# Two-layer hybrid backbone on one core: when weights are split, and when the mixer's residual is prepared

## The chip, the cores and the metric

One core of one Trainium2 chip runs the whole network in one launch. The metric is the device time of that launch in microseconds. Five engines work from queues of their own, each strictly in order: TensorE (PE; its weight loads are listed as PEld), VectorE (DVE), ScalarE (ACT), GpSimd (POOL) and SyncE (SP), whose queue issues all the DMA loads and stores of this kernel.

## The reference

A two-layer network over 512 latent tokens and 256 context tokens of width 1024, in float32. Layer 0 mixes with gated linear attention beside differential attention, layer 1 with a bidirectional state-space (SSD) mixer; each layer then has a SwiGLU feed-forward network (FFN) with 2816 hidden units. What matters here is the frame around the mixers:

```python
x = layer_norm(ALPHA * x + gm_x * mix_x, ln_g[layer, 0], ln_b[layer, 0])
x = layer_norm(ALPHA * x + gf_x * swiglu(x * (1.0 + scf_x) + shf_x, ffn_w_in[layer], ffn_w_out[layer]),
               ln_g[layer, 1], ln_b[layer, 1])
...
# end of the SSD mixer (layer 1; only latent tokens are needed there)
y = y.reshape(b, s, SSD_D_INNER) * jax.nn.silu(z.astype(F32))
return group_rms_norm(y, norm_w).astype(z.dtype) @ w_out
```

## The kernel before

**Products in three.** Each float32 matrix is kept as a high half (rounded to float32r, a form that TensorE multiplies faster) and a low half (the rest). A product is `mm3`: high by high, high by low, low by high. Activations are held in `R0` as such a pair, weights in `RW`. The weights are read from memory in 222 items of up to 128x1024, in the fixed order of the list `plan`. An item passes three stations:

- its load, a DMA of 512 KB, into one of three buffers of `RAW`;
- its *split*: ScalarE copies it into the high half (`RW<-RAW`, 128x1024), then VectorE or GpSimd subtracts that from the item to get the low half (`RW<-RAW,RW`);
- its use on TensorE, out of one of four buffers of `RW` (a pair of halves each).

`issue_loads` drives this. `wq` counts the items loaded, split (`issued`), `taken` by a step of the kernel and `freed` after their last product. An item may be loaded up to three ahead of the splits and split up to four ahead of what has been freed. In the kernel before, `issue_loads` runs at `free` alone, and it books every split that a free buffer allows at once. A step takes one item (a convolution's 128 columns, `cv`), two (a gate and up pair of the FFN, or the halves of `z`) or three or four (rows of an output matrix: `fo`, `ow`, `sw`).

**A planner orders the queues.** The kernel is not issued in program order. `Timing` keeps a clock for TensorE and, for VectorE (V), ScalarE (S), GpSimd (G), the DMA issues (Q) and the transfers (D), lists of booked stretches, with estimated costs. An operation is booked at the first room on its engine from the moment that its operands are ready, which may be up to 10 us before TensorE's clock; an L list keeps GpSimd apart from those VectorE operations that read two operands from SBUF. `either` books an elementwise operation on VectorE or GpSimd, wherever it ends sooner by the estimate. At `flush` all that was booked is issued in order of the planned time. So what is booked first gets the room, and what comes later in the program is placed around it. Every instruction is then listed under one line of the profile (L105), and tiles have to be told apart by names: `HB` is the big work buffer, `HX` and `l` (slots of the layer) hold smaller ones, `f` those of the FFN, `R` is the activations' pair, `PS` PSUM, `xres` the residual stream in memory, `acs_rows` the decay rows that layer 1 loads for every tile.

Dependent work beside the products runs as generators (`spawn`); `pump`, called after every `mm3`, advances those whose operands the planner holds ready, `need` those that must be done.

**Layer 1.** Its steps are written out by hand:

```python
ORDER1 = "b0 x0 z0 x1 z1 x2 b1 z2 x3 x4 o0 x5 z3 b2 z4 o1 z5 x6 b3 x7 z6 o2 p z7 o3"
```

`b` and `x` are projections with a convolution (B and C, or 256 channels of x), `z` the gate's projection of 256 columns, whose tanh and silu product (`SZ`) are booked at its end; `o` is a quarter of the output product over four tiles of 128 tokens, summed in `acc`. For each `x` a chain `y_tile` per tile builds the SSD output, gates it with `SZ`, and transposes it for `o`. `o3` does not sum but goes on, tile by tile, into the layer norm: `out_tile` calls `ln.last` (gate, add the prepared residual, statistics), then `ln.chain` normalizes, transposes and writes the tile into `R0` for FFN 1. What `ln.last` adds to is prepared by `ln.prep(t)`: load `x` of the tile from `xres` into a buffer (there is one for all four tiles), scale it by `ALPHA` on ScalarE, multiply `acc` by the gate, add the two. Those are two operations of 128x1024 in HB, both booked by `either`. In the kernel before, step `p` does this for all four tiles, ahead of `z7` and `o3`.

Of the kernel before, what the change touches and what calls it, by code (L numbers as in the profile page):

```python
# [15 lines left out]
ALU = mybir.AluOpType  # L16
# [8 lines left out]
NT = NTOK // P  # L25
# [193 lines left out]
def backbone(ctx: ExitStack, tc: tile.TileContext, ins: dict, out: bass.AP):  # L219
    nc = tc.nc  # L220
    tm = Timing(nc)
    V, S, G = tm.V, tm.S, tm.G
    dma = tm.dma
# [93 lines left out]
        return c  # L317

    def pump():
        going = True  # L320
        while going:
            going = False
            for c in list(chains):
                if c.ready <= tm.clock and c.can():
                    c.step()
                    going = True
                    break
# [35 lines left out]

    plan = []
    wgate = {}
    wq = {"loaded": 0, "issued": 0, "taken": 0, "freed": 0}
    wviews = {}

    def plan_cols(key, w, c0, n=P):
# [6 lines left out]
        for i in range(2):  # L376
            plan.append(((key, n, i), [(None, w[i * 512:(i + 1) * 512, c0:c0 + 256].rearrange("(k p) c -> p k c", p=P))], (4, 256)))

    def issue_loads(limit=None):
        limit = limit or len(plan)  # L380
        while wq["loaded"] < min(limit, wq["issued"] + 3):
            j = wq["loaded"]
            _, pieces, (a, b) = plan[j]
            rv = RAW[:, j % 3, 0:a * b].rearrange("p (a b) -> p a b", b=b)
            for sl, ap in pieces:
                dma(rv[:, :, sl] if sl is not None else rv, ap)
            wq["loaded"] += 1
        if wq["issued"] < min(limit, wq["freed"] + 4):
            j = wq["issued"]
            _, _, (a, b) = plan[j]  # L390
            r = RAW[:, j % 3, 0:a * b]
            i = j % 4
            hi, lo, hf = RW[:, i, 0:a * b], RW[:, 4 + i, 0:a * b], RWf[:, i, 0:a * b]
            if plan[j][0] in wgate:
                tm.either(r, r, wgate[plan[j][0]], ALU.mult)
            S.activation(hi, r, AF.Copy)
            tm.either(lo, r, hf, ALU.subtract)
            wviews[j] = hi.rearrange("p (a b) -> p a b", b=b), lo.rearrange("p (a b) -> p a b", b=b)
            wq["issued"] += 1
            issue_loads(limit)  # L400

    def take(key):
        j = wq["taken"]
        assert plan[j][0] == key, (plan[j][0], key)
        wq["taken"] += 1
        return wviews[j]

# [313 lines left out]
    def start(mslots):  # L721
# [19 lines left out]
        for q in range(2):  # L741
            load_x(q)
            for i in range(4 * q, 4 * q + 4):
                load_mod(i)
            if q == 0:
                for j in range(4):
                    src = mod_b[0, j % 2 * 1024:j % 2 * 1024 + 1024].rearrange("(h q c) -> q h c", h=2, q=2)[j // 2]
                    dma(MB[32 * j:32 * j + 2, :].rearrange("p (h c) -> p h c", h=2), src.partition_broadcast(2))
                for d in range(2):
                    dma(prm_r[106:110, d * 64:(d + 1) * 64], ins["gla_b_gate"][0, d].rearrange("(h c) -> h c", c=64))  # L750
                issue_loads(3)
        load_x(2)
        load_x(3)
        for i in range(8, len(slots)):
# [55 lines left out]
        for q in range(3):  # L810
            while quarter[0] <= q:
                need_one()
            if q == 2:
                tm.floor["Q"] = tm.busy["Q"][-1][1]
                issue_loads()
                gate_params()
                load_params()
# [549 lines left out]
    def layer1(lnin, lnc):  # L1367
# [385 lines left out]
        for op in ORDER1.split():  # L1753
# [8 lines left out]
            elif op == "p":  # L1762
                need(*xsc[7])
                scale_shift(1, 1, 2)
                ln.load_gates()
                for t in range(2, NT):
                    ln.prep(t)
            else:
                ws = [take(("sw", 4 * i + k)) for k in range(4)]
                for t in range(2, NT):  # L1770
                    need(mxs[2 * i + 1])
                    need(yc[2 * i, t], yc[2 * i + 1, t])
                    out_tile(i, ws, t, t == NT - 1)
                    if i == 3:
                        outs[t] = spawn(ln.chain(t))
                        outs[t].step()
# [56 lines left out]
```

## Time and profile before

| | us |
|---|---|
| median of 3 runs (lowest, highest) | 2034.73 (2030.9, 2034.9) |
| the profiled execution | 2033.6 |
| its span, first to last instruction | 2031.7 |
| PE busy | 1921.0 |
| DVE busy | 1352.5 |
| ACT busy | 783.8 |
| POOL busy | 224.5 |

The times of the profile are those of the profiled execution, counted from its first instruction. Its stages are: layer 0 to about 510 (its start to 85), FFN 0 to about 1078, layer 1 to about 1650, FFN 1 to the end. An engine that is not the last to be waited for may idle at no cost; PE's idle time is what a gain has to come from.

### The profile page before, as it was taken

Reading aid. Unit: us, or ns where it says so; the run is one execution under the profiler, and the core shown is the slowest. Engines: PE = TensorE matmul, PEld = TensorE weight load, DVE = VectorE, ACT = ScalarE, POOL = GpSimd, SP = SyncE. Lnnn points to the kernel's source line nnn. Section 1 sums busy time; section 2 is a strip of 40 time slices with the busy share of each in tenths; the row PEclk is TensorE's granted clock in tenths of the full one; section 3 lists DMA queues with packets and bytes.
Section 4 is the critical chain, followed back from the end, with each engine's and each line's share of the span. In section 5 each row is a group of like instructions: output and inputs, shape, how many; then the busy total and the mean of one; then the engine's idle time right before and its main releaser. Section 6 shows DMA issues by size and latency. Waiting matters only on the chain.

```text
span 2031.7 us, 27248 instructions
## 1 busy us (share of the span) xinstructions
PE 1921.0 (95%) x10660; PEld 1650.1 (81%) x10660; DVE 1352.5 (67%) x2065; ACT 783.8 (39%) x1494; POOL 224.5 (11%) x281
## 2 busy tenths in 40 slices
PE   7999999997899999999998999999899789999997
PEld 4878787966899989899886888788788678888886
DVE  4765645588815656666478988977978884444456
ACT  3523135445423122212135465655546443222232
POOL 0100000021300000000113321401102230000010
PEclk9999999999999999999998999999999799999999
DMA  8433411122424434434323432233333325333331
GB/s 284 126 126 115 138 42 32 53 63 73 147 72 145 137 113 147 134 114 154 105 78 101 105 91 87 73 89 89 102 96 94 116 82 173 97 103 94 94 119 58
DMA packets 233071, 216.37 MB, mean 107 GB/s; under 512 B 18869, under 2 KB 202807, under 8 KB 232943
## 3 DMA queue, kind: packets, MB, share of 16 engines
q1 hardware_dynamic: 232943, 214.64, 34.4%
q8 instruction: 83, 1.36, 0.3%
q14 instruction: 45, 0.37, 0.1%
HBM read 204.94 MB, written 9.67 MB: 106 GB/s over the span
## 4 chain that ended last, share of the span: by engine, by line
PE 75%; DVE 14%; issue 3%; DMA 3%; ACT 3%; POOL 1%; SPq 0%; POOLq 0%; DVEq 0%; ACTq 0%
PE PS L105 75%; DVE HB L105 8%; DVE RW L105 2%; ACT HB L105 2%; DVE l L105 1%; DMA HB<-acs_rows 1%; DVE LNS L105 1%; ACT RW L105 1%; DMA HB<-in_x_dram 1%; DVE HX L105 1%; DVE sml L105 0%; SPq L105 0%; POOL HB L105 0%; DVE R L105 0%; POOL LNS L105 0%
## 5 line engine op out<-in xcount | busy, mean ns | idle before, releaser
L105 PE MATMUL PS<-R,RW 128*128 128x384 f32 (+3 forms) x5184 | 987.3, 349 | 19.9 <-DVE HB L105 5.8
L105 PEld LDWEIGHTS PS<-R,RW 128*128 128x128 f32 (+1 forms) x5184 | 887.3, 189 | 106.0 <-issue 20.6
L105 DVE TENSOR_TENSOR RW<-RAW,RW 128x1024 fp32r<-128x1024 f32 (+1 forms) x204 | 255.8, 1270 | 217.4 <-ACT RW L105 216.7
L105 ACT ACTIVATE RW<-RAW 128x1024 fp32r<-128x1024 f32 (+1 forms) x222 | 228.8, 1046 | 237.5 <-issue 174.5
L105 PE MATMUL PS<-RW,f 128*128 128x512 f32 x1320 | 304.7, 390 | 1.9 <-DVE RW L105 1.5
L105 ACT ACTIVATE HB<-PS 128x512 f32<-128x512 f32 (+4 forms) x247 | 129.8, 533 | 428.0 <-PE PS L105 409.7
L105 PEld LDWEIGHTS PS<-RW,f 128*128 128x128 f32 x1320 | 247.0, 188 | 55.0 <-DVE RW L105 2.1
L105 DVE TENSOR_TENSOR HB<-PS,HB 128x512 f32<-128x512 f32 (+2 forms) x276 | 160.2, 587 | 92.3 <-PE PS L105 88.7
L105 PE MATMUL PS<-RW,R 128*128 128x256 f32 (+1 forms) x1440 | 200.7, 298 | 5.4 <-DVE HB L105 4.1
L105 ACT ACTIVATE HB<-HB 128x128 f32<-128x128 f32 (+4 forms) x372 | 159.9, 488 | 102.6 <-DVE HB L105 67.5
L105 PEld LDWEIGHTS PS<-RW,R 128*128 128x128 f32 x1440 | 186.8, 196 | 14.1 <-DVE HB L105 4.9
L105 PE MATMUL PS<-RW,l 128*128 128x512 f32 x576 | 157.5, 415 | 15.5 <-DVE HX L105 6.8
L105 DVE TENSOR_TENSOR HB<-HB 128x256 f32<-128x256 f32 (+3 forms) x191 | 151.2, 802 | 21.8 <-ACT HB L105 16.3
L105 PE MATMUL PS<-HB 128*128 128x128 f32 (+6 forms) x896 | 147.2, 353 | 10.2 <-DVE HB L105 7.6
L105 PEld LDWEIGHTS PS<-RW,l 128*128 128x128 f32 x576 | 105.1, 192 | 45.5 <-DVE HX L105 8.2
L105 PEld LDWEIGHTS PS<-HB 128*128 128x128 f32 (+3 forms) x896 | 100.9, 188 | 42.5 <-DVE HB L105 12.7
L105 ACT ACTIVATE f<-HB 128x384 fp32r<-128x384 f32 (+2 forms) x68 | 37.4, 550 | 236.5 <-DVE HB L105 236.4
L105 POOL TENSOR_TENSOR HB<-HB 128x256 f32<-128x256 f32 (+1 forms) x55 | 72.8, 1334 | 504.8 <-DVE HB L105 336.1
L105 DVE TENSOR_TENSOR HB<-HB,PS 128x384 f32<-128x384 f32 (+2 forms) x68 | 39.7, 584 | 106.2 <-PE PS L105 106.2
L105 DVE SCALAR_TENSOR_TENSOR HB<-HB,CST 128x1024 f32<-128x1024 f32 x84 | 105.0, 1277 | 0.0
L105 DVE SCALAR_TENSOR_TENSOR HB<-HB,CW 128x770 f32<-128x770 f32 (+1 forms) x96 | 102.0, 1066 | 3.0
L105 PE MATMUL PS<-ident,HB 128*128 128x128 f32 x480 | 76.8, 288 | 22.5 <-DVE HX L105 11.5
(145 smaller groups left out, 1297.8 us busy)
## 6 DMA issues: line engine op xcount, KB each, us to landing
RAW<-in_ffn_w_in_dram SPq DMA_DIRECT2D x88, 512.0 KB
HB<-in_mod_w_dram SPq DMA_DIRECT2D x48, 512.0 KB
RAW<-in_ffn_w_out_dram SPq DMA_DIRECT2D x44, 512.0 KB
RAW<-in_ssd_w_in_dram SPq DMA_DIRECT2D x40, 512.0 KB
mod<-in_mod_w_dram SPq DMA_DIRECT2D x72, 256.0 KB
HB<-acs_rows SPq DMA_DIRECT2D x64, 256.0 KB
RAW<-in_ev_w_in_dram SPq DMA_DIRECT2D x20, 512.0 KB
RAW<-in_ssd_w_out_dram SPq DMA_DIRECT2D x16, 512.0 KB
```

The source lines that it names most:

```text
L105: f(*a, **k)
```

## The change

Two things change. First, `issue_loads` is also called by every `pump` and by `take`, and a split is booked only if `idle` finds, on the planner's lists, that VectorE has room for the low half by the time that the high half is done, or by now. Whatever `idle` says, an item is booked if it is one of the next two to be taken, and `take` books its own item. The limit of items (three during the start) becomes a field of `wq`. The loads are issued in the same function, so they follow the splits. Second, `ln.prep(t)` of layer 1's mixer moves from step `p`, where it stood for all four tiles, into `o3`, ahead of each tile's `out_tile`.

```diff
     def pump():
+        issue_loads()
         going = True
...
-    def issue_loads(limit=None):
-        limit = limit or len(plan)
-        while wq["loaded"] < min(limit, wq["issued"] + 3):
...
-        if wq["issued"] < min(limit, wq["freed"] + 4):
+    def idle(r, hi, lo):
+        n = math.prod(r.shape[1:])
+        c = [tm.COST[e][0] + tm.COST[e][1] * n for e in "SV"]
+        t = tm.room("S", max(tm.ready(r, 1), tm.free(hi, 1), tm.clock - 10.0), c[0]) + c[0]
+        t = max(t, tm.free(lo, 1))
+        return tm.room("V", t, c[1], True) <= max(t, tm.clock) + 0.1
+
+    def issue_loads(upto=0):
+        limit = wq["limit"]
+        while True:
+            while wq["loaded"] < min(limit, wq["issued"] + 3):
...
             j = wq["issued"]
+            if j >= min(limit, wq["freed"] + 4):
+                return
...
+            if j >= max(upto, wq["taken"] + 2) and not idle(r, hi, lo):
+                return
-            if plan[j][0] in wgate:
-                tm.either(r, r, wgate[plan[j][0]], ALU.mult)
+            if key in wgate:
+                tm.either(r, r, wgate[key], ALU.mult)
             S.activation(hi, r, AF.Copy)
             tm.either(lo, r, hf, ALU.subtract)
...
             wq["issued"] += 1
-            issue_loads(limit)
 
     def take(key):
         j = wq["taken"]
+        issue_loads(j + 1)
         wq["taken"] += 1
         return wviews[j]
...
                 ln.load_gates()
-                for t in range(2, NT):
-                    ln.prep(t)
             else:
                 ws = [take(("sw", 4 * i + k)) for k in range(4)]
                 for t in range(2, NT):
                     need(mxs[2 * i + 1])
                     need(yc[2 * i, t], yc[2 * i + 1, t])
+                    if i == 3:
+                        ln.prep(t)
                     out_tile(i, ws, t, t == NT - 1)
```

More of the change, by code (lines that the diff above doesn't have):

```diff
@@ L365, in backbone @@
     wgate = {}
-    wq = {"loaded": 0, "issued": 0, "taken": 0, "freed": 0}
+    wq = {"loaded": 0, "issued": 0, "taken": 0, "freed": 0, "limit": 0}
     wviews = {}
@@ L377, in plan_halves @@
             plan.append(((key, n, i), [(None, w[i * 512:(i + 1) * 512, c0:c0 + 256].rearrange("(k p) c -> p k c", p=P))], (4, 256)))
-    def issue_loads(limit=None):
-        limit = limit or len(plan)
-        while wq["loaded"] < min(limit, wq["issued"] + 3):
[L382 to L387, printed above, removed]
-        if wq["issued"] < min(limit, wq["freed"] + 4):
+    def idle(r, hi, lo):
[8 more added lines that the diff above has]
+            while wq["loaded"] < min(limit, wq["issued"] + 3):
+                j = wq["loaded"]
+                _, pieces, (a, b) = plan[j]
+                rv = RAW[:, j % 3, 0:a * b].rearrange("p (a b) -> p a b", b=b)
+                for sl, ap in pieces:
+                    dma(rv[:, :, sl] if sl is not None else rv, ap)
+                wq["loaded"] += 1
             j = wq["issued"]
-            _, _, (a, b) = plan[j]
+            if j >= min(limit, wq["freed"] + 4):
+                return
+            key, _, (a, b) = plan[j]
             r = RAW[:, j % 3, 0:a * b]
@@ L750, in start @@
                     dma(prm_r[106:110, d * 64:(d + 1) * 64], ins["gla_b_gate"][0, d].rearrange("(h c) -> h c", c=64))
-                issue_loads(3)
+                wq["limit"] = 3
+                issue_loads()
         load_x(2)
@@ L814, in start @@
                 tm.floor["Q"] = tm.busy["Q"][-1][1]
+                wq["limit"] = len(plan)
                 issue_loads()
```

## The prediction, before the run

> **What bounds the kernel now.** The page's first part comes first, then busy time by stage (the windows view, columns: stretch, its length, then busy time and count of PE, PEld, DVE, ACT and POOL, granted clock, DMA share, GB/s).
>
> ```profile
> PE 1921.0 (95%) x10660; PEld 1650.1 (81%) x10660; DVE 1352.5 (67%) x2065; ACT 783.8 (39%) x1494; POOL 224.5 (11%) x281
> ...
> 85.00:470.00 385.00, 367.42 (x2315) 297.76 (x2315) 250.57 (x473) 149.07 (x314) 30.27 (x32) 0.97 0.29 89
> 585.00:1040.00 455.00, 455.00 (x2441) 424.21 (x2440) 261.07 (x292) 114.42 (x156) 10.76 (x6) 1.00 0.40 125
> 1040.00:1165.00 125.00, 112.36 (x624) 95.52 (x623) 111.74 (x148) 58.15 (x104) 31.24 (x37) 0.96 0.32 91
> 1165.00:1610.00 445.00, 416.79 (x2424) 357.15 (x2422) 379.87 (x660) 249.82 (x581) 93.27 (x152) 0.97 0.31 91
> 1672.00:1972.00 300.00, 300.00 (x1361) 250.00 (x1361) 128.61 (x142) 84.81 (x106) 7.51 (x3) 1.00 0.36 110
> ```
>
> TensorE is busy for 95% of the span, so at most 2031.7 - 1921.0 = 110.7 us of idle time, and what the lower clock beside it costs, are to be had. The two FFN bodies (585 to 1040 and 1672 to 1972) have PE without a pause at full clock: nothing that moves work of DVE or ACT can gain there. The idle time to work on lies in layer 0 (17.6 us of 385), at the end of FFN 0 (12.6 of 125) and in layer 1 (28.2 of 445, with DVE busy for 85%), and past it up to FFN 1. Of all gaps one is by far the largest, and it stands where the second part of the change works: between `z7` and `o3`, the last two steps of layer 1. First the stages around it, then the timeline (start, length, engine, operation, output<-inputs, idle time before and its releaser).
>
> ```profile
> 1575.00:1603.00 28.00, 25.24 (x153) 22.59 (x151) 25.48 (x41) 11.79 (x20) 8.97 (x6) 0.88 0.30 95
> 1603.00:1614.00 11.00, 0.25 (x3) 0.05 (x1) 10.18 (x15) 3.77 (x7) 4.47 (x3) 0.63 0.60 174
> 1614.00:1652.00 38.00, 33.26 (x152) 25.71 (x153) 30.47 (x62) 17.43 (x43) 10.12 (x11) 0.93 0.14 47
> ```
>
> ```profile
> 1584.66 3.46 DVE L105 TENSOR_TENSOR HB<-HB,HX 128x512 f32<-128x512 f32 x2
> 1584.68 2.90 POOL L105 TENSOR_TENSOR HB<-HB 128x1024 f32<-128x1024 f32 x1
> 1588.67 3.41 DVE L105 TENSOR_TENSOR RW<-RAW,RW 128x1024 fp32r<-128x1024 f32 x2
> 1592.00 0.74 DVE L105 SCALAR_TENSOR_TENSOR HB<-PS,RS,HB 128x512 f32<-128x512 f32 x1
> 1592.79 7.63 PE L105 MATMUL PS<-RW,R 128*128 128x256 f32 x39 [2.58 <-DVE HB L105]
> 1593.58 4.82 DVE L105 TENSOR_TENSOR HB<-HB 128x1024 f32<-128x1024 f32 x4
> 1602.20 2.49 DVE L105 TENSOR_TENSOR HB<-HB 128x1024 f32<-128x1024 f32 x1 [1.63 <-ACT HB L105]
> 1604.25 0.58 ACT L105 ACTIVATE HX<-PS 128x512 f32<-128x512 f32 x1
> 1604.62 0.68 DVE L105 TENSOR_TENSOR HB<-PS,HB 128x512 f32<-128x512 f32 x1
> 1604.74 0.46 SPq L105 DMA_DIRECT2D HB<-xres  x1
> 1605.13 2.34 POOL L105 TENSOR_TENSOR RW<-RAW,RW 128x1024 fp32r<-128x1024 f32 x1
> 1605.40 2.81 DVE L105 TENSOR_TENSOR HB<-HB 128x256 f32<-128x256 f32 x2
> 1609.37 0.89 DVE L105 TENSOR_TENSOR HB<-HB 128x256 f32<-128x256 f32 x2
> 1610.23 2.23 ACT L105 ACTIVATE HB<-HB 128x1024 f32<-128x1024 f32 x5 [5.40 <-DMA HB<-xres]
> 1611.32 1.23 DVE L105 TENSOR_TENSOR HB<-HB 128x1024 f32<-128x1024 f32 x1 [0.48 <-ACT HB L105]
> 1612.46 0.68 DVE L105 SCALAR_TENSOR_TENSOR l<-l,PS 128x512 f32<-128x512 f32 x1
> 1613.06 0.68 DVE L105 SCALAR_TENSOR_TENSOR HX<-HX,PS 128x512 f32<-128x512 f32 x1
> 1613.65 0.75 DVE L105 SCALAR_TENSOR_TENSOR l<-HB,l 128x256 f32<-128x256 f32 x2
> 1614.13 0.69 PE L105 MATMUL PS<-ident,l 128*128 128x128 f32 x2 [10.88 <-DVE l L105]
> 1614.70 0.36 SPq L105 DMA_DIRECT2D HB<-acs_rows  x1
> 1617.03 1.23 DVE L105 TENSOR_TENSOR HB<-HB 128x1024 f32<-128x1024 f32 x1 [1.31 <-ACT HB L105]
> ```
>
> Read it backwards. PE stands still for 10.88 us until 1614.13, for the transposes of the gated `y`, which need the silu products of `z7` (the two at 1612.46 and 1613.06). ScalarE had the second bank's tanh done at 1604.25 + 0.58 = 1604.83; the products came 7.6 us later because DVE takes its queue in order. Ahead of them stand seven 128x1024 operations in HB that belong to `ln.prep`: one on POOL at 1584.68, four on DVE from 1593.58, one at 1602.20 and one at 1611.32; an eighth follows at 1617.03. Three of the DVE ones make DVE wait for the scaled residual first, whose load (1604.74) landed just before 1610.23.
>
> **Part by part: the residual by tiles.** `p` loses four loads of 512 KB on SP's queue, four scalings on ACT and eight operations; `o3` gains the same, two operations before each tile. Nothing is added.
>
> (a) The gap before `o3`. Gone from ahead of the silu products are 4.82 + (1.63 + 2.49) + (0.48 + 1.23) = 10.65 us of DVE time. The gain is bounded by the tanh: products at 1604.9 and 1605.5, the gating 0.6 later, PE 0.48 after that starts (as 1613.65 stands to 1614.13), hence 1606.6 for 1614.13, at most 7.5 us. What stays on DVE, the tile work from 1604.62 to 1610.8, is some 6 us, of which 2.81 - 0.89 = 1.9 is the wait beside POOL's split at 1605.13; part of it can go earlier into the time that comes free from 1593.58. Bounds 0 and 7.5; I take 5.5, near the upper end, as more is removed than the bound needs.
>
> (b) The gap of 2.58 us in `z7` ends with the product at 1592.00, behind 3.46 us for two 512-wide operations beside POOL's 2.90 us residual product, and 3.41 us for two splits. A split alone is 1.22 (the row of 1303.13 below), so the two lose 0.97 there. Bounds 0 and 2.58; 1.5, since the slow pair goes but the splits stay.
>
> (c) `o3` pays. Tiles 3 to 5 bring six operations of 1.23 (the row of 1617.03) into 1614 to 1652; one is there already, so 5 x 1.23 = 6.15 us. DVE has 38.00 - 30.47 = 7.5 us free there, in pieces shorter than one operation between waits. Half absorbed: a loss of 3 (bounds 0 and 6.15; the rival below goes further). Tile 2's pair can run before `o3`, in what (a) leaves free. The loads still form a chain through one buffer: issue 1604.74 to ACT 1610.23 is 5.5 us, ACT 1.07 by the row quoted last below, DVE 1.23: 7.8 us, a tile of `o3` takes some 9 (38 us for four), so the load stays covered; were it not, its tile would wait for the difference. On SP's queue these loads come to stand among those of `acs_rows` (one is issued at 1614.70), which a tile's ScalarE work waits for; what that gives or takes lies within the bounds of (c).
>
> (d) The clock is 0.63 in the gap and 0.93 in the 38 us after it. A shorter gap leaves less to run slow: 0.07 x 33.26 = 2.3 us is the most; I take 0.5. The Trainium skill (TensorE: Matmul & The Clock Gate, What's actually happening) says the clock halves after an idle window of about 3.4 us; the trace agrees that it falls with this gap, and by the rule a gap left below that would save up to 1.7 us, for 2025.5.
>
> **The splits.** Before, a split was booked as soon as its buffer was free, at the first room on DVE. Now the third and fourth item ahead wait while DVE has bookings past the end of the high half; the next two are always forced. First, for 1165 to 1610, the busy time of instructions on the tile RW alone and DVE's waits; then rows of the timeline and, last, one of the chain that ended last.
>
> ```profile
> 1165.00:1610.00 445.00, 325.02 (x1770) 268.84 (x1768) 52.85 (x42) 46.50 (x45) 7.13 (x3) 0.97 0.31 91
> ...
> DVE RW L105 <- ACT RW L105: 16.3, 18, 1.8
> ...
> 1461.42 1.06 ACT L105 ACTIVATE RW<-RAW 128x1024 fp32r<-128x1024 f32 x1 [1.88 <-PE PS L105]
> 1468.79 2.35 DVE L105 TENSOR_TENSOR RW<-RAW,RW 128x1024 fp32r<-128x1024 f32 x2
> 1471.89 1.41 PE L105 MATMUL PS<-R,RW 128*128 128x256 f32 x8 [3.79 <-DVE l L105]
> 1090.11 4.50 DVE L105 TENSOR_TENSOR RW<-RAW,RW 128x1024 fp32r<-128x1024 f32 x2
> 1094.99 1.33 PE L105 MATMUL PS<-ident,HB 128*128 128x128 f32 x5 [4.60 <-DVE HX L105]
> 1303.13 1.22 DVE L105 TENSOR_TENSOR RW<-RAW,RW 128x1024 fp32r<-128x1024 f32 x1
> 1303.70 1.67 PE L105 MATMUL PS<-RW,l 128*128 128x512 f32 x4
> 1610.23 1.07 ACT HB L105
> ```
>
> In layer 1 DVE does 42 splits; 18 times it stood idle until the high half came (the waits row). For these DVE was free, and nothing changes. Where it was busy, the split counts only if PE soon waits behind it. Clearest is 1468.79: high half ready at 1462.5, low halves 6.3 us later, 2.35 us just ahead of the `z5` products on which PE waits 3.79 us. These two are third and fourth ahead, so they may go behind: 2.3 us. The pair at 1090.11, 4.50 us ahead of a gap of 4.60, is in the buffers of `cv20` and `cv0`, the next two once `dt` and `cv16` are taken, so forced at about the same moment: 0, with 4.5 as its bound. Lesser ones, with layer 0, I put at 1.2. In FFN two items are in use and the next two forced, or three in use and one ahead: 0; PE's full 455 us covers it, and a split that came late would cost up to its 1.22. Lateness elsewhere: at `o0` the last split ended at 1304.35, and PE's pause at it is below one (1.67 us for the four products at 1303.70); two more such stops a `take` of four would cost 2 to 5 us over four steps. Loads move with their splits (RAW is freed by them) and pass the `acs_rows` loads on SP. Sum 3.5, bounds -5 and 9.
>
> **Sum:** 5.5 + 1.5 - 3.0 + 0.5 + 3.5 = 8.0 us. The profiled execution took 2033.6 us (span 2031.7 and 1.9 around it), so 2025.6; it lies 1.1 under the median of the runs, 2034.73, so 2026.7 for a median.
>
> **Rivals.** *`o3` turns DVE-bound (slower).* Place: 1614 to 1652, DVE at 80% already. Price: each of tiles 3 to 5 puts two operations and a wait for the scaled residual in front of its layer norm, 3 x (1.23 + 1.23 + 1.31) = 11.3, less 2.5 that stand there now: 8.8. Where the planner gives the products to POOL, DVE's two-input operations stretch as at 1605.40, 1.9 each: 5.7 more. 14.5 against (a) and (b), 7.0, gives +7.5, so 2042; with the splits' gain 2039. It decides once a tile loses over 3.7 us (11 / 3). For it: DVE was already last at nearly each step of `o3`; against: its 7.5 us free and the eighth operation, which is there now. The Trainium skill (SBUF — State Buffer, Who interferes with whom) states this stretch as a rule: a DVE instruction with two SBUF inputs and a GpSimd one that reads SBUF block each other for a whole instruction. The trace agrees (2.81 for 0.89).
>
> *Nothing comes of it.* DVE's work from 1575 to 1652 is the same; `z7` gets shorter and `o3` longer by as much, and the splits stood well. (a) + (b) - 6.15 is then about 1: 2034 with some 3 either way.
>
> *More.* The bounds of (a), (b) and the pair at 1090.11: 7.5 + 2.6 - 3 + 0.5 + 8 = 15.6, so 2019, and down to 2015.
>
> **Chances.** Two runs of this kernel tell 0.2% (4.1 us) apart. The forecast 0.48, more 0.12: together 0.60 for faster. Nothing 0.20: same. The slower rival 0.17, and 0.03 for splits that come late at the `take` of four: 0.20. The forecast's own range is 2020 to 2030; 2015 to 2039 leaves out the slower rival's upper half and some of more, 2 in 10.
>
> **What would show it.** The gap before `o3` at 3 to 6 us with no 128x1024 operation in HB ahead of the silu products; two such a tile inside `o3`, and `o3` 2 to 4 us longer; the gap at `z5` near 1.5; FFN bodies as long as now. Wrong it would be if those operations stretch on DVE or run on POOL within `o3`, if ACT waits there for `xres`, or if PE begins to wait on DVE RW at the `take` of four.

## The result, and the profile after

The changed kernel took 2049.12 us (median of 4 runs, 2047.07 to 2051.35); the kernel before, run beside it, 2033.23. The ratio is 1.0079, with an interval of 1.0061 to 1.0097: 16 us slower where 8 faster was forecast. The profiled execution has a span of 2049.1 us, 17.4 over that of before.

First the page's part 1 of the changed kernel.

```profile
PE 1928.2 (94%) x10660; PEld 1656.7 (81%) x10660; DVE 1361.6 (66%) x2040; ACT 784.2 (38%) x1494; POOL 286.7 (14%) x306
```

The same operations ran, but 25 of them have gone from VectorE (2065 before) to GpSimd (281 before), and yet VectorE is busy for 9 us longer, not shorter. GpSimd is busy for 62 us more. The windows view of the stages, shifted by what each starts later:

```profile
85.00:470.00 385.00, 367.38 (x2321) 297.92 (x2320) 249.51 (x469) 148.77 (x314) 44.01 (x38) 0.97 0.29 90
585.00:1048.00 463.00, 463.00 (x2488) 432.21 (x2487) 263.38 (x294) 116.28 (x159) 10.74 (x6) 1.00 0.40 124
...
1173.00:1628.00 455.00, 419.14 (x2433) 358.65 (x2432) 389.35 (x652) 252.10 (x590) 126.34 (x165) 0.97 0.30 89
1690.00:1990.00 300.00, 300.00 (x1359) 249.89 (x1359) 128.77 (x142) 84.70 (x106) 7.50 (x3) 1.00 0.36 111
```

Layer 0's row differs from that of before in GpSimd alone (44 us for 30). The FFN bodies have PE without a pause, as before. Layer 1's stretch is 10 us longer for nearly the same PE work, with GpSimd busy for 126 us and not 93. Of its instructions on the tile RW alone, with the same columns:

```profile
1173.00:1628.00 455.00, 325.59 (x1775) 268.46 (x1773) 39.11 (x31) 46.75 (x45) 38.91 (x15) 0.97 0.30 89
```

and from the waits view of that stretch (total, times, longest):

```profile
DVE RW L105 <- ACT RW L105: 17.4, 14, 3.9
```

VectorE does 31 low halves there (42 before), 14 of them (18 before) after standing idle for the high half; GpSimd does 15 (3 before). Last, the timeline between `z7` and `o3`:

```profile
1611.61 4.91 POOL L105 TENSOR_TENSOR HB<-HB 128x1024 f32<-128x1024 f32 x2
1621.87 1.23 DVE L105 TENSOR_TENSOR RW<-RAW,RW 128x1024 fp32r<-128x1024 f32 x1 [0.52 <-ACT RW L105]
1623.15 1.22 DVE L105 TENSOR_TENSOR RW<-RAW,RW 128x1024 fp32r<-128x1024 f32 x1
1624.29 0.68 DVE L105 SCALAR_TENSOR_TENSOR l<-l,PS 128x512 f32<-128x512 f32 x1
1624.88 0.68 DVE L105 SCALAR_TENSOR_TENSOR HX<-HX,PS 128x512 f32<-128x512 f32 x1
1625.95 0.69 PE L105 MATMUL PS<-ident,l 128*128 128x128 f32 x2 [6.94 <-DVE l L105]
1636.50 5.18 POOL L105 TENSOR_TENSOR HB<-HB 128x1024 f32<-128x1024 f32 x2 [1.25 <-ACT HB L105]
```

No residual product stands ahead of the silu products on VectorE any more, as forecast; the gap is 6.94 us and not 10.88. What stands there now is two low halves. Seven of the eight residual products run on GpSimd, within `o3` too (VectorE has one, at 1626.49).

**Where the time went.** For each kernel the trace gives the start of TensorE's first product with each weight. The table has the time from one such start to the next, less the same in the kernel before. The last column runs to the start of the last product. (The time up to `fu0.0`, the second item of FFN 0, and FFN 1 are left out of the columns but are in the last one. The first ranged from -4.6 to +2.2 us over kernels whose layer 0 is planned exactly as before, so it is scatter of a single profile; FFN 1 lies between -1.5 and +1.3.) `fu0.0` to `fg0.1` is the end of layer 0's last layer norm; `fg0.1` to `cv2` is FFN 0 and the first steps of layer 1; `sw12` is the first weight of `o3`, `fg1.0` the first of FFN 1.

| kernel | median us | ratio (interval) | `fu0.0` to `fg0.1` | to `cv2` | `cv2` to `z3` | `z3` to `sw12` | `o3` | whole |
|---|---|---|---|---|---|---|---|---|
| the change | 2049.12 | 1.0079 (1.0061, 1.0097) | +8.2 | 0.0 | +10.2 | -6.6 | +6.8 | +17.4 |
| residual_only | 2035.43 | 1.0013 (1.0001, 1.0025) | 0.0 | +0.1 | +0.8 | -7.7 | +7.3 | +2.7 |
| splits_only | 2052.30 | 1.0089 (1.0076, 1.0103) | +8.1 | +0.6 | +10.7 | +0.7 | -0.4 | +19.7 |
| after_low_dve | 2055.27 | 1.0108 (1.0093, 1.0122) | +0.3 | +16.5 | +10.2 | -9.8 | +8.3 | +22.2 |
| before_low_dve | 2038.82 | 1.0024 (1.0014, 1.0034) | +0.6 | +4.7 | -1.6 | +1.5 | +3.8 | +7.7 |
| defer_first | 2044.88 | 1.0057 (1.0037, 1.0078) | +8.2 | 0.0 | -0.3 | -5.8 | +8.8 | +8.7 |
| defer_l1 | 2042.84 | 1.0044 (1.0028, 1.0061) | 0.0 | 0.0 | +10.0 | -7.0 | +8.1 | +9.6 |
| horizon3 | 2039.96 | 1.0037 (1.0023, 1.0051) | +3.7 | 0.0 | +4.7 | -7.3 | +7.9 | +5.7 |
| before_loads2 | 2039.30 | 1.0039 (1.0026, 1.0052) | 0.0 | +0.9 | -0.5 | +3.2 | +4.6 | +6.2 |
| residual_pool | 2038.82 | 1.0023 (1.0013, 1.0032) | 0.0 | +0.5 | +3.3 | -8.4 | +10.0 | +3.2 |
| defer_not_tail | 2046.16 | 1.0073 (1.0057, 1.0089) | +1.4 | +0.2 | +12.1 | -7.3 | +7.4 | +12.5 |
| defer_z5 | 2034.61 | 1.0002 (0.9991, 1.0014) | -0.1 | +1.6 | +0.1 | -5.5 | +4.7 | +1.0 |
| residual_half | 2033.07 | 1.0002 (0.9991, 1.0013) | 0.0 | 0.0 | -0.1 | -4.4 | +3.1 | +0.8 |
| defer_l1_nolow | 2037.16 (one run) | | -0.2 | +1.6 | +8.1 | -8.0 | +7.7 | +3.6 |
| residual_nolow | 2037.19 (one run) | | 0.0 | -0.1 | +5.7 | -8.2 | +6.2 | +3.9 |
| residual_noprep | 2023.26 | 0.9946 (0.9933, 0.9958) | 0.0 | +0.1 | 0.0 | -12.2 | +2.6 | -11.9 |
| residual_fused | 2028.41 | 0.9971 (0.9960, 0.9981) | 0.0 | 0.0 | +0.5 | -11.3 | +5.0 | -3.1 |
| fused_z5 | 2024.85 | 0.9955 (0.9941, 0.9969) | 0.0 | +0.1 | +0.2 | -11.1 | +2.0 | -11.6 |
| before_cost | 2049.78 | 1.0077 (1.0058, 1.0097) | -2.2 | +2.6 | +10.7 | +1.4 | +5.2 | +15.9 |

### The profile page after: what moved, and what is told of

It is laid out like the page before. It is cut to its first block, busy times and chain, and to the rows that moved or that the text cites. A ratio compares the mean times of both kernels' runs of the same rounds, so it can differ in the third digit from the quotient of the medians.

```text
span 2049.1 us, 27253 instructions
## 1 busy us (share of the span) xinstructions
PE 1928.2 (94%) x10660; PEld 1656.7 (81%) x10660; DVE 1361.6 (66%) x2040; ACT 784.2 (38%) x1494; POOL 286.7 (14%) x306
## 4 chain that ended last, share of the span: by engine, by line
PE 71%; DVE 19%; ACT 3%; issue 3%; DMA 2%; POOL 1%; SPq 0%; POOLq 0%; DVEq 0%; ACTq 0%
PE PS L105 71%; DVE HB L105 13%; ACT HB L105 2%; DVE RW L105 2%; DVE l L105 1%; DVE LNS L105 1%; DVE sml L105 1%; DVE HX L105 1%; DMA HB<-in_x_dram 1%; DMA HB<-acs_rows 1%; ACT RW L105 1%; POOL LNS L105 0%; SPq L105 0%; DVE R L105 0%; POOL HB L105 0%
## 5 line engine op out<-in xcount | busy, mean ns | idle before, releaser
L105 DVE TENSOR_TENSOR RW<-RAW,RW 128x1024 fp32r<-128x1024 f32 (+1 forms) x187 | 236.0, 1276 | 223.2 <-ACT RW L105 222.1
L105 DVE TENSOR_TENSOR HB<-HB 128x256 f32<-128x256 f32 (+3 forms) x186 | 156.3, 848 | 19.9 <-ACT HB L105 13.8
L105 POOL TENSOR_TENSOR HB<-HB 128x256 f32<-128x256 f32 (+1 forms) x60 | 87.0, 1458 | 497.1 <-DVE HB L105 339.3
L105 PEld LDWEIGHTS PS<-RW,l 128*128 128x128 f32 x576 | 110.0, 199 | 45.1 <-DVE HX L105 5.1
L105 PEld LDWEIGHTS PS<-HB 128*128 128x128 f32 (+3 forms) x896 | 101.3, 186 | 40.1 <-issue 10.3
L105 POOL TENSOR_TENSOR RW<-RAW,RW 128x1024 fp32r<-128x1024 f32 (+1 forms) x35 | 89.3, 2553 | 218.4 <-ACT RW L105 210.0
L105 DVE SCALAR_TENSOR_TENSOR HB<-HB,CW 128x770 f32<-128x770 f32 (+1 forms) x96 | 116.0, 1211 | 4.7 <-ACT HB L105 1.3
```

Source lines behind the costliest of these rows:

```text
L105: f(*a, **k)
```

## The experiments

### The two parts, each alone

`residual_only` is the kernel before with the second part of the change, `splits_only` the changed kernel without it:

```diff
# residual_only, against before         # splits_only: the reverse, against after
                 ln.load_gates()
-                for t in range(2, NT):
-                    ln.prep(t)
...
+                    if i == 3:
+                        ln.prep(t)
                     out_tile(i, ws, t, t == NT - 1)
```

> The kernel before with the second part of the change alone (the residual prepared tile by tile in o3; splits as before). If the residual's move is the gain that the trace of after shows between z7 and FFN 1 (weights of sw12 were used 12.9 us earlier against sw11, o3 then lost 6.8), the time is 6 to 8 us under the kernel before, some 2026. If the move is what made the change slower (the prediction's rival of a DVE-bound o3), it is slower than before by 5 us or more.

> The changed kernel with the residual back in step p for all four tiles: the first part of the change alone. If the splits carry the whole loss, 2050 to 2058 us (the 16 us of the change and the 6 to 8 that the residual's move gives back). If the residual's move carries it, about 2033 as before.

The residual alone makes no difference that counts (1.0013). It gains 7.7 us up to `o3`, and `o3` gives back 7.3. The splits alone carry the whole loss, in two places: 8.1 us at the end of layer 0's layer norm, 10.7 between `cv2` and `z3`.

### Is it GpSimd's share of the low halves?

`after_low_dve` is the changed kernel and `before_low_dve` the kernel before with every low half on VectorE:

```diff
-            tm.either(lo, r, hf, ALU.subtract)
+            V.tensor_tensor(lo, r, hf, ALU.subtract)
```

> The changed kernel with every low half on VectorE (after has 35 of them on GpSimd, before 18). Theory A: the late splits cost because the planner, finding VectorE booked, gives their low halves to GpSimd, where each blocks VectorE's two-input operations: then most of the loss goes and the time is 2030 to 2040. Theory B: they cost by where they stand in the queues, whichever engine does them: then it stays at 2045 to 2055.

> The kernel before with every low half on VectorE (18 of 222 move there from GpSimd): the control for the run above. Theory A: a GpSimd low half costs more than it saves before the change too, so the same or up to 5 us faster, 2028 to 2034. Theory B: within 3 us of before, to either side.

Keeping GpSimd out of it does not cure the loss: 1.0108 against 1.0024, so the deferral costs as much without GpSimd. (The control is 5 us slower than the kernel before, more than either theory had.) The loss changes its form. The low halves now come late on VectorE, and TensorE waits for them, as in `o0`, by the timeline of `after_low_dve`:

```profile
1338.15 1.22 PE L105 MATMUL PS<-RW,l 128*128 128x512 f32 x2 [7.19 <-DVE RW L105]
```

### Where the deferral costs

The deferral is confined to part of the plan's 222 items: to layer 0, its layer norm and FFN 0 (`defer_first`), to layer 1 (`defer_l1`), or to the fourth item ahead (`horizon3`). Where no item is deferred, the order of work is that of `residual_only`: in `defer_l1`, GpSimd, TensorE and the DMA queue go through the same instructions in the same order up to 1084 us. `before_loads2` leaves the splits as before and makes the loads late.

```diff
# defer_first (j < 99), defer_l1 (99 <= j < 156), against after
-            if j >= max(upto, wq["taken"] + 2) and not idle(r, hi, lo):
+            if j < 99 and j >= max(upto, wq["taken"] + 2) and not idle(r, hi, lo):
# horizon3, against after
+            if j >= max(upto, wq["taken"] + 3) and not idle(r, hi, lo):
# before_loads2, against before
-        while wq["loaded"] < min(limit, wq["issued"] + 3):
+        while wq["loaded"] < min(limit, wq["issued"] + 2):
```

> The changed kernel with the splits of layer 0, of its layer norm and of FFN 0 deferred (the first 99 items of the plan) and all later ones placed at once, as before; the residual comes tile by tile. Theory P (a deferred split is booked behind what the two-input engines already have, in layer 0's layer norm and in layer 1): the 7 us at the first `fg`/`fu` items of FFN 0 stay lost, the 10 us of layer 1 do not come; with the residual's +1.6 it ends near 2042 (2038 to 2045). Theory L (loads that follow the deferred splits come late, wherever they are): layer 0 shows waits of ACT on RAW, and a time above 2045. Theory N (any reordering of this plan costs some us, by chance): no particular place, anywhere from 2034 to 2050.

> The changed kernel with only layer 1's splits deferred (items 99 to 155 of the plan), those of layer 0 and both FFNs placed at once; residual tile by tile. Theory P: equal to the kernel before up to the end of FFN 0, then the 10 us between `cv2` and `z2` are lost again; with the residual's +1.6 near 2045 (2041 to 2049). The sum of this run's and the last one's excess over the kernel before is that of the changed kernel (+16) plus the residual's +1.6 counted twice. Theory L: the same place, but with ACT waiting for RAW ahead of the gaps. Theory N: the loss stands elsewhere in layer 1 than in the changed kernel, or is gone.

> The changed kernel with a split forced one item earlier (the next three are placed at once, only the fourth may wait). Theory P: fewer splits stand behind booked work, so between the changed kernel and the one with the residual alone: about 2041 (2036 to 2046), with less lost at the start of layer 1 and ahead of FFN 0. Theory L: loads come about one split earlier than in the changed kernel; also between, no distinction by the time, but the gaps would go with ACT's waits on RAW. Theory N: no order among the three kernels.

> The kernel before with each weight's load issued one split later (two loaded ahead of the last split and not three); the splits are placed as before. This makes the loads late without deferring a split. Theory L: the loss of the changed kernel comes with it, 2044 to 2055. Theory P: loads have room; within 5 us of the kernel before (2031 to 2039), with no loss between `cv2` and `z2`.

The two places are independent: 8.2 us come with the first deferral, 10.0 with the second, each without the other's. Forcing one item earlier about halves both (3.7 and 4.7). Late loads cost 6 us, but elsewhere: nothing at the layer norm, -0.5 between `cv2` and `z3`. So theory L falls for these two places.

### The layer norm at the end of layer 0

Here the rows show the cause. The timeline of the kernel before:

```profile
516.38 2.35 DVE L105 TENSOR_TENSOR RW<-RAW,RW 128x1024 fp32r<-128x1024 f32 x2
...
520.96 1.22 DVE L105 TENSOR_TENSOR RW<-RAW,RW 128x1024 fp32r<-128x1024 f32 x1
...
523.87 7.97 POOL L105 TENSOR_TENSOR HB<-HB 128x1024 f32<-128x1024 f32 x3
527.18 1.09 PE L105 MATMUL PS<-ident,HB 128*128 128x128 f32 x8 [1.17 <-DVE HX L105]
```

and of the changed kernel:

```profile
517.12 1.21 DVE L105 TENSOR_TENSOR RW<-RAW,RW 128x1024 fp32r<-128x1024 f32 x1
...
522.46 8.40 POOL L105 TENSOR_TENSOR HB<-HB 128x1024 f32<-128x1024 f32 x3
525.31 6.63 DVE L105 TENSOR_TENSOR RW<-RAW,RW 128x1024 fp32r<-128x1024 f32 x2
...
532.32 1.97 PE L105 MATMUL PS<-ident,HB 128*128 128x128 f32 x8 [7.75 <-DVE HX L105]
```

Before, the low halves of the second `fg`/`fu` pair were done by 522.2, ahead of GpSimd's three products. Deferred, they were forced together, fell beside these products and took 6.63 us for 2.4; behind them in VectorE's queue stood the last tile's steps out of PSUM (at 531.86), and TensorE waited 7.75 us for them. `defer_not_tail` takes the deferral away from these four items alone:

```diff
+            if not 33 <= j <= 36 and j >= max(upto, wq["taken"] + 2) and not idle(r, hi, lo):
```

> The changed kernel with the four items at layer 0's last layer norm (the first two `fg`/`fu` pairs of FFN 0) placed at once, all others deferred as in the changed kernel. If the 7 us lost there come from this pair, forced late beside GpSimd's products of that layer norm: 16 - 7, near 2042 (2039 to 2046), with PE's use of the second pair within 2 us of the kernel before. If they come from what was shifted earlier in layer 0 (`ow4` to `ow7` come 5 to 9 us later in the changed kernel), the 7 us stay: 2047 to 2051.

There the loss falls from 8.2 to 1.4 us, so the deferral of these items is its cause. (With every low half on VectorE, in `after_low_dve`, this place costs 0.3, and 16.5 are lost behind FFN 0 instead, at `z0`.) The time falls by less than the 7 expected, by 4.9 us between the two profiles and by 3 between the medians (2046.16; the intervals of the two ratios overlap), in part because layer 1, planned anew behind it, loses 12.1 and not 10.2 between `cv2` and `z3`.

### The start of layer 1

The stretch from `cv2` to `z3` in three kernels that have the residual by tiles. Windows of all instructions of `residual_only`, then of those on RW alone; likewise `defer_l1`:

```profile
1146.80:1364.40 217.60, 204.81 (x1177) 175.12 (x1176) 190.68 (x315) 127.88 (x291) 51.63 (x86) 0.98 0.31 85
```

```profile
1146.80:1364.40 217.60, 159.11 (x843) 130.38 (x842) 23.86 (x19) 21.54 (x21) 6.21 (x2) 0.98 0.31 85
```

```profile
1145.40:1372.23 226.83, 204.93 (x1177) 174.40 (x1175) 196.69 (x308) 129.04 (x290) 66.78 (x91) 0.98 0.29 82
```

```profile
1145.40:1372.23 226.83, 156.30 (x843) 128.48 (x841) 14.85 (x12) 21.95 (x21) 24.30 (x9) 0.98 0.29 82
```

TensorE's busy time is the same; its idle time grows from 12.8 to 21.9 us. VectorE lost seven low halves (23.86 to 14.85 us), but all else that it does takes 196.69 - 14.85 = 181.8 us, not 190.68 - 23.86 = 166.8, at 296 instructions in both: 15 us of stretching beside GpSimd. `residual_pool` puts nine low halves on GpSimd as well, but at their old places:

```diff
-            tm.either(lo, r, hf, ALU.subtract)
+            if j == 105 or 110 <= j <= 118 and j != 117:
+                G.tensor_tensor(lo, r, hf, ALU.subtract)
+            else:
+                tm.either(lo, r, hf, ALU.subtract)
```

> The kernel before with the residual tile by tile (2035.4, 1.6 over the kernel before), no split deferred, but nine low halves of layer 1 given to GpSimd: those of `z0` (second half), `cv4`, `cv5`, `cv17`, `cv21`, `z2` (both), `cv6` and `cv8`, which stand on GpSimd in the changed kernel and on VectorE in this one's base. Theory E (layer 1's loss between `cv2` and `z3` comes from GpSimd's reads beside VectorE's two-input operations, the late placing only being what sends the halves there): the same 10 us are lost there, 2045 (2041 to 2049), DVE's 128x770 operations at 1.3 us mean and not 1.17. Theory P (the place in the queue costs by itself): 2033 to 2039, with no more than 3 us lost there.

Its rows, all instructions and RW alone:

```profile
1144.03:1364.10 220.07, 204.93 (x1176) 175.77 (x1175) 186.86 (x304) 128.65 (x292) 76.18 (x98) 0.98 0.32 88
```

```profile
1144.03:1364.10 220.07, 158.75 (x842) 129.99 (x841) 13.85 (x11) 21.72 (x21) 25.64 (x10) 0.98 0.32 88
```

VectorE's other work: 173.0 us, a stretch of 6 and not 15 (some 7, as three instructions fewer stand in it), though GpSimd does more. The loss is 3.3 us, near theory P: at their old places the halves on GpSimd cost 2.5 us more than the run without them, where the deferral costs 9.2 more. Two more kernels leave these nine low halves out, with and without the deferral in layer 1 (`defer_l1_nolow`, `residual_nolow`); `before_cost` changes nothing but one number of the planner:

```diff
# defer_l1_nolow, against defer_l1; residual_nolow, against residual_only
-            tm.either(lo, r, hf, ALU.subtract)
+            if not (j == 105 or 110 <= j <= 118 and j != 117):
+                tm.either(lo, r, hf, ALU.subtract)
# before_cost, against before
-        "V": (0.15, 1.06e-3, 0.03, 0.06),
+        "V": (0.15, 1.07e-3, 0.03, 0.06),
```

> The kernel with only layer 1's splits deferred, and nine low halves left out (the second half of `z0`, `cv4`, `cv5`, `cv17`, `cv21`, both of `z2`, `cv6`, `cv8`): seven of them stood on GpSimd and two on VectorE. `cv2` to `z3` took 226.8 us with them, 217.6 without the deferral. Theory E (the loss is where the late low halves fall): 212 to 217, within 3 us of the run beside it. Theory Q (the rest of the order, ScalarE's high halves or the loads): 220 to 226, still 7 us or more above the run beside it.

> The control: no split deferred, residual by tiles, the same nine low halves left out (all on VectorE, 9 x 1.23 = 11 us of its time). `cv2` to `z3`: 217.6 with them; 210 to 216 without, as VectorE is busy for 88% of this stretch and PE for 94%.

> The kernel before with the planner's cost of VectorE for each element raised from 1.06 to 1.07 ns: the same work by the same rules, only planned a little otherwise. Theory N (the plan of before came out well in layer 1, and any other costs some us): `cv2` to `z3` 3 to 6 us longer, the time 2037 to 2043. Theory E alone (only late splits cost): within 2 us everywhere, 2032 to 2036.

Both expectations on the halves missed. Without the nine, the deferral still loses 8.1 us here, and the control, with 11 us less for VectorE to do, loses 5.7. The difference between the two has fallen from 9.2 to 2.4, as theory E has it, but by the control's growing worse. And `before_cost`, with no deferral at all, loses 10.7 us in this stretch and 16 in all, more than theory N had. Its windows rows for the stretch, all instructions and RW alone, and its longest gap there:

```profile
1144.16:1371.63 227.47, 205.71 (x1176) 175.18 (x1175) 191.36 (x316) 128.48 (x291) 51.22 (x85) 0.95 0.29 82
```

```profile
1144.16:1371.63 227.47, 157.03 (x842) 129.32 (x841) 19.51 (x16) 21.63 (x21) 13.45 (x5) 0.95 0.29 82
```

```profile
1259.39 1.54 PE L105 MATMUL PS<-ident,HB 128*128 128x128 f32 x6 [9.22 <-DVE HB L105]
```

Set beside the rows of `residual_only`: the same busy time on every engine, within 1 us, and 9 us more idle time of TensorE. So a plan of this stretch has a price of its own that no engine's busy time shows. The mix is not quite the same: five low halves stand on GpSimd and not two, and VectorE's other work takes 171.9 us for 166.8 (with four instructions more). Nor is the loss the same one. TensorE's delay behind the kernel before, counted from `cv2`, at the start of four steps:

| kernel | `z2` | `cv6` | `o0` | `z3` |
|---|---|---|---|---|
| the change | +18.3 | +10.2 | +15.3 | +10.2 |
| defer_l1 | +18.3 | +10.9 | +25.0 | +10.0 |
| before_cost | +3.5 | +10.3 | +16.6 | +10.7 |

The deferral loses its time ahead of `z2` (in the change in seven waits for VectorE, 12.6 us in all and 4.4 the longest, where the kernel before has 3.7 us of waits), and part of it is made good by `cv6`; `before_cost` loses most of it in the one gap ahead of `cv6`. Over the kernels whose splits are not deferred there, the change of the whole stretch stands at -1.6, -0.5, -0.3, -0.1, 0.0, +0.1, +0.2, +0.5, +0.8, +3.3, +5.7 and +10.7; most of the nine near zero have the order of before there. With the deferral it is 4.7, 8.1, 10.0, 10.2, 10.2, 10.7 and 12.1. **What stays open:** how much of layer 1's 10 us belongs to late splits as such, and how much to the loss of an order that had come out well. The stretch beside GpSimd is seen in the changed kernel, but a loss as large came with a third of it, at another place. `before_cost` shows how much a plan alone can cost; it does not show that the change lost its time in that way.

### The one gain that the prediction priced in detail

`defer_z5` defers only `cv19` and `cv23`, whose low halves stood ahead of the `z5` products, and keeps these on VectorE, with the residual in `p` as before:

```diff
# defer_z5, against splits_only
-            if j >= max(upto, wq["taken"] + 2) and not idle(r, hi, lo):
+            if 140 <= j <= 141 and j >= max(upto, wq["taken"] + 2) and not idle(r, hi, lo):
                 return
...
-            tm.either(lo, r, hf, ALU.subtract)
+            if 140 <= j <= 141:
+                V.tensor_tensor(lo, r, hf, ALU.subtract)
+            else:
+                tm.either(lo, r, hf, ALU.subtract)
```

> The kernel before, residual in `p`, with just two splits deferred (`cv19` and `cv23`, those that stand ahead of the `z5` products at 1468.79) and their low halves kept on VectorE. This is the one place where the prediction priced a gain of the deferral in detail. If that step was right: the gap of 3.79 us at `z5` falls to about 1.5 and the time by 2.3, to 2031 (2029 to 2033). If layer 1 is bound by VectorE's work there, so that an order within it only moves the wait: the gap falls, the next ones grow, and the time stays within 2 us of the kernel before or above it. In the changed kernel the gap was 3.54, with `cv19`'s low half on GpSimd.

The timeline of `defer_z5`, and then of the changed kernel at the same place:

```profile
1472.21 1.31 PE L105 MATMUL PS<-R,RW 128*128 128x256 f32 x9 [1.52 <-DVE l L105]
```

```profile
1485.18 2.52 POOL L105 TENSOR_TENSOR RW<-RAW,RW 128x1024 fp32r<-128x1024 f32 x1
1485.54 2.90 DVE L105 TENSOR_TENSOR HB<-HB 128x256 f32<-128x256 f32 x2
...
1489.64 2.90 PE L105 MATMUL PS<-R,RW 128*128 128x256 f32 x12 [3.54 <-DVE l L105]
```

Alone, the gap falls from 3.79 to 1.52 us, as worked out, and the time from `z5`'s first product to `cv19`'s by 3.8. In the changed kernel the planner gave `cv19`'s half to GpSimd instead; the two VectorE operations beside it took 2.90 us (0.88 in the kernel before, at 1467.53), and the gap stayed at 3.54. Even alone the gain is gone by FFN 1: the time is that of before (1.0002).

### What `o3` is bound by

`residual_half` prepares two tiles in `p` and two in `o3`. `residual_noprep` is `residual_only` without the two products of `prep`, which it leaves out. `residual_fused` computes the mixer's residual in another order, with three passes over a tile on VectorE and GpSimd for four, no scaling on ScalarE, two buffers for the residual, and nothing but two loads in `p`:

```diff
# residual_fused, against before, in last() (and prep() for this layer norm only loads)
+            if r is not None:
+                V.scalar_tensor_tensor(y, o, r, y, ALU.mult, ALU.add)
+                tm.either(y, y, self.gate[0][:, c], ALU.mult)
+                V.scalar_tensor_tensor(y, self.xr[t % len(self.xr)][:, c], ALPHA, y, ALU.mult, ALU.add)
...
-                for t in range(2, NT):
+                for t in range(2, 4):
                     ln.prep(t)
...
                     out_tile(i, ws, t, t == NT - 1)
+                    if i == 3 and t + 2 < NT:
+                        ln.prep(t + 2)
```

> The kernel before with the residual of tiles 2 and 3 prepared in `p`, of tiles 4 and 5 in `o3` ahead of their tile. With all four in `o3` the time before `o3` fell by 8.3 us and `o3` gave back 7.3. If both go by the number of tiles: 4 gained, 3.7 lost, no change (2031 to 2037). If `o3` has room for two tiles but not for four (7.5 us of VectorE's time were free there): 4 gained, 1 lost, 2030 to 2031, better than both kernels. If what is left of the gap does not shrink, since a tile's products still stand ahead of the silu products: 2034 to 2038.

> The kernel with the residual by tiles, no split deferred (2035.4), that leaves out the product of `y` with the gate and the sum with the scaled residual in layer 1's mixer (its loads and its scaling stay). Theory V (`o3` is bound by VectorE's work): `o3` no longer gives back the 7 us, so 2028 (2025 to 2030). Theory O (`o3` gives them back through its order: the chain of loads, the waits for the scaled residual, the normalisation of each tile): 2033 to 2036.

> The kernel before with the mixer's residual computed in another order: `out*r + y` first, then times the gate, then plus ALPHA times the residual in one VectorE operation, per half tile; no scaling on ScalarE, three passes over a tile on VectorE and not four, none of them ahead of `o3`; two buffers for the residual, loaded two tiles ahead. Theory V: the gap before `o3` goes (8 us), `o3` pays about half of what four passes cost, and the three passes behind each bank add about 2 x 0.7 per tile to the chain: 2029 to 2032. Theory O: nothing or a loss, since a bank's result now has three operations in front of the layer norm: 2034 to 2040.

`fused_z5` is `residual_fused` with the two deferred splits of `defer_z5`.

> The kernel with the residual in three passes (2028.4) and the two deferred splits ahead of `z5`. If the 3.8 us gained there were lost again because `o3` was bound by VectorE's work: they are kept in part now, 2025 to 2028. If they are lost between `z6` and `z7`, in the new order there: 2028 to 2033.

The windows of `o3` (from `sw12` to `fg1.0`) in the kernel before, in `residual_only`, `residual_noprep`, `residual_fused` and `fused_z5`, and of `residual_only` a row of its timeline:

```profile
1614.47:1649.33 34.86, 31.21 (x140) 23.87 (x139) 27.37 (x58) 17.12 (x43) 8.74 (x11) 0.93 0.14 48
```

```profile
1608.65:1650.82 42.17, 33.90 (x141) 26.31 (x139) 33.45 (x59) 19.11 (x45) 22.87 (x16) 0.86 0.25 81
```

```profile
1599.94:1637.41 37.47, 31.57 (x141) 24.95 (x140) 27.02 (x59) 19.16 (x45) 8.72 (x11) 0.91 0.24 77
```

```profile
1605.60:1645.50 39.90, 33.08 (x140) 25.73 (x139) 30.09 (x64) 16.04 (x42) 8.97 (x11) 0.88 0.23 72
```

```profile
1600.43:1637.27 36.84, 29.48 (x141) 22.15 (x139) 32.55 (x66) 16.86 (x40) 8.99 (x11) 1.00 0.24 81
```

```profile
1615.98 7.87 POOL L105 TENSOR_TENSOR HB<-HB 128x1024 f32<-128x1024 f32 x3
```

In `residual_only` the planner put the residual products on GpSimd (POOL 22.87 us and not 8.74). VectorE runs 59 instructions, as many as without them and nearly the same, in 33.45 us and not 27.02: 6.4 us of stretching, and `o3` is 4.7 us longer than without the products. Taking the products away altogether gives 12 us in all (2023.26 against 2035.43), more than expected: the profiles show 4.7 in `o3` and 4.5 ahead of it, about the 8 x 1.23 = 9.8 us of the products, so these are on the path. So theory V holds for 4.7 of the 7.3 us that `o3` gave back; what makes the other 2.6 stays open. `residual_half` goes by the number of tiles: 4.4 us gained ahead of `o3`, 3.1 given back in it, no change in the time. The order with three passes brings a gain clear of the noise: 2028.41 us, and with the two splits 2024.85. Both beat the two kernels; their own intervals overlap. Whether the pass less brings it, the scaling that ScalarE no longer does or the second buffer was not tested apart.

In `fused_z5` TensorE's gap ahead of `o3` is gone (none is over 1.3 us in its timeline from 1600 on up to 1637), the granted clock in `o3` is 1.00 and its busy time there 29.48 us for the 31.21 to 33.90 of the others. Of the 3.8 us gained at `z5` nothing shows in `z3` to `sw12` (-11.1 against -11.3 without the two splits); what is gained shows in `o3`, 3.0 us, which is about the 3.6 us that the clock gives. That the two splits brought the clock about is read from these two profiles alone; the one of `fused_z5` is of its fastest execution (2021.71 us, mean clock 0.984, the five others 0.979 to 0.982).

## Why the prediction was wrong, point by point

**The splits: the step that failed.** Its term was +3.5 with bounds -5 and 9; measured alone it is -18 (1.0089 of 2033.82), and in the change, against `residual_only`, -13 (0.0066 of 2033). What the runs show in its place: some 8 us lost at layer 0's last layer norm, where two forced low halves ran beside GpSimd's products, and some 10 in layer 1, whose share between late halves and the new order stays open. Three parts of the step failed.

- "For these DVE was free, and nothing changes." Of the 42 low halves on VectorE in layer 1, the prediction looked at where VectorE was free when the half was made, and not at what the planner does with a half that it books after everything else. A half booked last finds the room taken: it goes to GpSimd (15 and not 3) or behind other work. The prediction had the price in its own rows (2.81 us for 0.89 beside GpSimd's split), and used it only for `o3`. The rule behind it (the Trainium skill, SBUF — State Buffer, Who interferes with whom), which the prediction named there, is borne out here as well: 6.63 us for two halves beside GpSimd's products.
- "Lesser ones, with layer 0, I put at 1.2." The pair forced at layer 0's last layer norm cost 8.2 us. The bound of -5 for late splits was thought of as stops at the `take` of four. Those came, within the bound: 0.6 us on VectorE's low halves in `o1`, and in `o0` 4.0 us on a high half and on a low half that GpSimd made (the two rows below). But TensorE was 15.3 us behind when `o0` began, counted from `cv2`, and at the layer norm the wait came behind the late halves, in VectorE's queue.

```profile
1327.33 0.73 PE L105 MATMUL PS<-RW,l 128*128 128x512 f32 x1 [1.92 <-ACT RW L105]
1330.12 1.22 PE L105 MATMUL PS<-RW,l 128*128 128x512 f32 x2 [2.06 <-POOL RW L105]
```

- The 2.3 us at `z5` were worked out rightly, for a plan that moves these two splits and nothing else. The planner moved everything behind them too. That a plan costs something of its own was nowhere in the sum, and `before_cost` shows that it can be as large as the whole result.

**(a) and (b), the time ahead of `o3`.** Right in the mechanism and in the sum: no residual product stands ahead of the silu products, and of 7.0 us forecast 7.7 came in `residual_only`. The parts are off: `z7`'s products take 3.1 us less (16.6 for 19.7; (b) had 1.5), the time from them to `o3` 5.2 less (9.25 for 14.41). The gap itself falls by 3.4 us, to 7.47, and to 6.94 in the change, where (a) had a fall of 5.5 and 3 to 6 us left. Two low halves stand directly ahead of the silu products in both kernels (2.4 us of VectorE's time), in the room that the residual left; in `residual_only`:

```profile
1604.38 2.35 DVE L105 TENSOR_TENSOR RW<-RAW,RW 128x1024 fp32r<-128x1024 f32 x2
1606.64 0.68 DVE L105 SCALAR_TENSOR_TENSOR l<-l,PS 128x512 f32<-128x512 f32 x1
...
1608.31 0.69 PE L105 MATMUL PS<-ident,l 128*128 128x128 f32 x2 [7.47 <-DVE l L105]
```

**(c), `o3` pays.** Mis-sized: -3 with a bound of -6.15; measured -7.3 in `residual_only` and -6.8 in the change. It was worked out as six products on VectorE. They went to GpSimd (in the change one stayed on VectorE), and it was VectorE's other work that stretched, as the slower rival had it (8.8 us and 5.7 for the stretch; 7.3 is what came). ScalarE did not wait for `xres` in `o3`; its wait for `acs_rows` there grew from 1.6 to 2.2 us, and to 3.8 in the change.

**(d), the clock.** Forecast +0.5. In `residual_only` it went the other way: granted 0.86 in `o3` and not 0.93, TensorE's busy time 33.90 and not 31.21 us, so -2.7, within the 7.3 above. A gap of 7.47 us was still long enough. Where the gap went, in `fused_z5`, the clock was 1.00 and 1.7 us were saved against before. That is the value which followed from the rule of the Trainium skill (TensorE: Matmul & The Clock Gate, What's actually happening) for a gap under 3.4 us. The trace agrees that the clock falls with the gap, but not that it takes a gap of 3.4 us: in the kernel before, the granted clock was 0.51 from 1592 to 1599, about the gap of 2.58 us, and in `residual_fused` 0.50 from 1614.5 to 1617.9, behind one of 1.99 us. Nor does the clock over `o3` go by the length of the gap ahead of it: 0.93 after 10.88 us, 0.86 after 7.47, 0.88 after 3.94. The two windows rows:

```profile
1592.00:1599.00 7.00, 6.21 (x29) 6.21 (x30) 6.79 (x14) 0.00 (x0) 0.55 (x1) 0.51 0.59 191
```

```profile
1614.50:1617.90 3.40, 3.40 (x13) 3.04 (x13) 2.73 (x4) 0.00 (x0) 0.00 (x0) 0.50 0.22 81
```

**The rivals.** "Nothing comes of it" was right for the residual alone, for its own reason: `z7` gets shorter and `o3` longer by as much. "`o3` turns DVE-bound" had the mechanism of (c), but its price is not what made the change slower. No rival had a loss from the splits away from a `take` of four, and the time lies 7 us above the highest that any of them gave (2042).

## What to carry to other kernels

To put an operation off until its engine is idle is also to book it last: on an engine that is busy for most of the time (85% in layer 1) it then falls beside the busiest work, or goes to the engine that slows the first. Ask of each operation put off what will have taken its room, and what stands behind it in the queue when it comes. Where a planner orders the work, re-plan the old kernel with a one per cent change before reading a loss or a gain of that size as the effect of an idea; and where a stage is bound by one engine's work, take a pass away from it rather than move it.

## What the runs showed of the hardware

A VectorE operation with two inputs from SBUF, 1.22 us alone, took 3.3 us for each of two beside three GpSimd products back to back (6.63 us for the pair): each was held up by 2.1 us, most of a GpSimd product (8.40 / 3 = 2.8). And the price of low halves on GpSimd lay in where they fell more than in their number: against the two of `residual_only`, the nine of `defer_l1` stretched VectorE's other work by 15 us, the ten of `residual_pool` by 6 to 7.
